# First loads of the down product moved into the last up pair, rotations moved beside the gates, six stores moved to ScalarE's queue

## The chip, the cores and the metric

The kernel runs on one core of one Trainium2 chip. The metric is the device time of one execution in microseconds (us), as the median of several runs; less is better. PE is TensorE (matmuls), PEld its weight loads, DVE is VectorE, ACT ScalarE, POOL GpSimd, and SP (SyncE) mostly issues DMAs. ACT can issue DMAs too, each in its own order of instructions. Every engine runs its instructions in order, so an instruction that waits holds up those behind it.

## The reference

One hybrid decoder block, float32, 1024 rows of width 1024 (SiLU feed-forward width 2816). Cut to what matters:

```python
h = x + 0.5 * swiglu(rms_norm(x, g1), w1a, w3a, w2a)      # (silu(x @ w1) * (x @ w3)) @ w2
u = rms_norm(h, g2)
q, k, v, p, gate_logits = split(u @ w_in)                 # one input projection, 3*768 + 512 + 2048 wide
yA = dilated_window_attention(rope(q), rope(k), v) @ w_A  # 3 groups of 4 heads, dilations 1, 4, 16
yB = pooled_minus_token(p) @ w_B                          # trailing means over 2, 4, 8, 16 rows
h = h + (sigmoid(gA) * yA + sigmoid(gB) * yB) @ w_o
h = h + 0.5 * swiglu(rms_norm(h, g3), w1b, w3b, w2b)
return rms_norm(h, g4)
```

The rotation (rope) touches the first 16 of the 64 entries of a head.

## The kernel before

**Number format and product.** Every float32 factor is split in two parts, hi and lo (ACT copies hi, DVE or POOL subtracts for lo), and a product is three matmuls: hi*hi, lo*hi, hi*lo. On top of that every large product is done in quadrants with seven products instead of eight. In the stages up and mix the seven are called m = 1, 6, 2, 7, 5, 4, 3 (`ORDER`), an item is 12 matmuls of 128x512, and products 1 and 2 share one PSUM bank, as do 5 and 3 (`Quad.run`, `Sevens.product`, L312). Sums of weights are made on DVE (`Quad.operand`, L343 to L354) and split two items ahead (`Sevens.split`, L301 on ACT, L304 on DVE or POOL).

**Weights.** `Stream` (`raws`) loads pieces of weights in one order through SP (L67, L69) into a ring of buffers `raw`; `raws.get()` takes the next and `raws.back(n)` gives n back and at once issues the loads that now have room.

**Stages.** up of the first FFN (to 457 us of the profile), down (to 680), entry and mix (684 to 1082), attention (to 1210), the product with w_o (to 1296), entry, up and down of the second FFN (1296 to 1989).

**Up and down.** `up` multiplies pairs of width blocks by w1 and w3; `Pair.a_out` and `b_out` empty the banks (b_out on DVE, L514 to L524) and `finish` spills five sums of the gated result to DRAM (`gs`, L533 on SP). `Down` multiplies these by w2 in steps of 24 matmuls: `load` fetches a spilled sum (`g`, L610, SP), `begin` takes raw weights, sums them (L646, DVE) and splits weights (`b`) and activations (`a`) (L625 on ACT; L629 on DVE, each fourth on POOL), `multiply` is L663. In `run`, step i is followed by load i+3 and begin i+2. At the end of `up`, load 0, begin 0, load 1 and begin 1 stand after the last item and before the last spills, load 2 after them.

**Mix.** 19 blocks of columns of the input projection (`MIX`), seven items each: blocks 0 to 8 are queries, keys and values, 9 and 12 pooling, 10, 11 and 13 to 18 gates. A loop over items k runs product k, then empties the bank of item k-1 in `Mix.out` (L926 to L947): of one block, DVE does m = 7 in L935 and m = 5 in L939, and product 3, two items after 5, accumulates into the bank that L939 reads. Gates end with a sigmoid on ACT (L947). What follows a block (`finish`) is a generator in the list `later`; each yield gives the number of items to wait. For queries and keys it is `rotate`: stores to DRAM on ACT's queue (`rot`, `qk`), a load of the part that is rotated (`ro`, L970), a shuffle (L974), a product with a table on POOL (L975) and one on DVE (L976), their sum (L980) and a store (L982). For gates it is `store` (L956, SP). With block 12 the tables are dropped and the attention's mask is loaded.

**Attention and w_o.** Near the end of mix the attention's inputs are fetched (`qk_in`, `pool_in`, L1547, in rings on SP). At the end of w_o, the rows h are stored to `h_dram[1]` (L1878, SP), squared on ACT (L257), and overwritten by DVE with their scaled form (L265), transposed on PE (`x_b`, L379) and split for the second FFN.

Of the kernel before, what the change touches and what calls it, by code (L numbers as in the profile page):

```python
# [27 lines left out]
GROUPS = 3  # L28
# [81 lines left out]
MIX = []  # L110
# [16 lines left out]
def tile_block(  # L127
# [31 lines left out]
    def sbuf(name, side="left", bufs=1):  # L159
        return tc.tile_pool(name=name, bufs=bufs, side=side, reuse_waits="tile")  # L160
# [156 lines left out]
    class Quad:  # L317
# [36 lines left out]
                ve.tensor_tensor(src, a12, self.s2, op=OP.subtract)  # L354
            self.w[m] = self.sv.split(src, f"{n}{m}", eng)

        def run(self, m):
            if m not in self.w:
                self.operand(m)
            w, n = self.w.pop(m), self.n  # L360
            x = {1: "b11", 2: "b21", 3: "b22", 4: "t4", 5: "t1", 6: "t2", 7: "t3"}[m]
            key = {1: "x", 2: "x", 5: "v", 3: "v"}.get(m, m)
            if m not in (2, 3):
                self.bank[key] = bank("mm" if key in ("x", "v") else "acc", f"u_{self.sv.name}{n}{m}")
            self.sv.product(self.bank[key], w, x, start=m not in (2, 3))
            if m == 3:
                raws.back(2)
            return self.bank[key]

# [15 lines left out]
    class Entry:  # L385
# [19 lines left out]
        def then(self, i):  # L405
            if i is not None:
                self.out(i)
# [139 lines left out]
            spill(6, d[:, highs])  # L547
            spill(5, d[:, lows])

    def up(sv, sums, between, at_end, begun):  # L550


        for j in range(NPAIR - 1):
            ms = [m for m in ORDER if j not in begun or m not in (1, 2)]
            q = begun.pop(j, None) or Pair(sv, j, sums)
            for m in ms:
                q.a(m)
            raws.depth = 4
            if j == NPAIR - 2:
                between()  # L560
            for m in ms[:-2]:
                q.b(m)
            if j == NPAIR - 2:
                end = Pair(sv, NPAIR - 1, sums)
                for m in ORDER[:2]:
                    end.A.operand(m)
            for m in ms[-2:]:
                q.b(m)
            q.finish()
        with tc.manual_schedule():  # L570
            items = [(w, m, out) for w, out in ((end.A, end.a_out), (end.B, end.b_out)) for m in ORDER]
            n = len(items)
            res = []
            for k, (w, m, out) in enumerate(items):
                if k + 2 < n:
                    items[k + 2][0].operand(items[k + 2][1])
                res.append(w.run(m))
                if k == n - 1:
                    then = at_end(sv.half_tile)
                if k > 0:  # L580
                    items[k - 1][2](items[k - 1][1], res[k - 1])
            then()
            end.b_out(ORDER[-1], res[-1])
            end.finish()

    def spilled(name):
        return [
# [4 lines left out]
    class Down:  # L592

        def __init__(self, name, sums, dp):
            self.name, self.sums, self.dp = name, sums, dp
            self.steps = [(m, s) for m in range(len(DOWN)) for s in range(len(PAIRS))]
            self.held, self.g, self.ops, self.banks = {}, {}, {}, {}
            self.n_lo = 0  # L600
            self.half_tile = None

        def size(self, i):
            js = PAIRS[self.steps[i][1]]
# [25 lines left out]
                at += n  # L630
            return hi, lo

        def begin(self, i):
            m, s = self.steps[i]
            pr = DOWN[m]
            size = self.size(i)
            for kn in pr.loads:
                self.held[kn, s] = raws.get()
            if len(pr.right) == 1:
                srcs = [self.held[pr.right[0], s]]  # L640
            else:
                x, y, op = pr.right
                srcs = []
                for a in range(size):
                    t = self.half_tile("s", f"w{i}_{a}").rearrange("p (a c) -> p a c", a=1)
                    ve.tensor_tensor(t, self.held[x, s][:, a:a + 1], self.held[y, s][:, a:a + 1], op=op)  # L646
                    srcs.append(t)
            w = self.split("b", srcs, i)
            for kn in pr.drops:
                del self.held[kn, s]  # L650
            raws.back(len(pr.drops))
            self.ops[i] = (self.split("a", [self.g.pop(i)], i), w)

        def multiply(self, i, t):
# [15 lines left out]
        def run(self, pool, after, tick=None):  # L670
            def half_tile(tag, n):
                return pool.tile([P, HALF], F32, tag=tag, bufs=4, name=f"{tag}_{self.name}{n}")

            self.half_tile = half_tile
            self.load(2)
            n = len(self.steps)
            done = []
            for i, (m, s) in enumerate(self.steps):
                if i < n - 2:
                    for t in range(4):  # L680
                        self.multiply(i, t)
# [159 lines left out]

    sums = spilled("f1")
    mstack, dstack = ExitStack(), ExitStack()
    down = []
    X_mix = {}

    def begin_down1(half_tile):
        scope.close()
        X_mix.update(sums_of_x(mstack.enter_context(sbuf("xa")), "mix", ("b21", "b11")))
        return begin_down("f1", half_tile)  # L850

    def begin_down(name, half_tile):
        d = Down(name, sums, dstack.enter_context(sbuf(f"down_{name}")))
        down.append(d)
        d.half_tile = half_tile
        d.load(0)
        d.begin(0)

        def then():
            d.load(1, row)  # L860
            d.begin(1)

        return then

    def load_residual():
        for t in range(NT):
# [7 lines left out]
    with sbuf("up1", "right") as fp:  # L874
        sv1 = Sevens("f1", X, fp)
        with tc.manual_schedule():
            begun = begin_up1()
        up(sv1, sums, load_residual, begin_down1, begun)
    raws.depth = RAW_BUFS


# [25 lines left out]
    class Mix:  # L907
# [44 lines left out]

        def store(self):
            yield 2
            for a in range(2):
                nc.sync.dma_start(gate_dram[self.g][:, a], self.y[a])  # L956

        def rotate(self):
            g, y = self.g, self.y
# [3 lines left out]
            for a in range(2):  # L963
                for n in range(2):
                    nc.scalar.dma_start(given[:, a, n].rearrange("t r c -> r t c"),
                                        y[a][n * HD:n * HD + 16].rearrange("r (t c) -> r t c", t=2))
                nc.scalar.dma_start(qk_dram[u][a].rearrange("h d c -> (h d) c"), y[a])
                yield 1 + a
            ro = tmp(f"ro{u}").rearrange("p (a c) -> p a c", a=2)
            nc.scalar.dma_start(ro[:, 0, :], given.rearrange("t a h r c -> (t a h r) c"))  # L970
            yield 2
# [30 lines left out]
        def window(self):  # L1002

            yield 1
            for a in range(2):
# [34 lines left out]
                for part, v in enumerate((hi, lo)):  # L1040
                    nc.sync.dma_start(pool_dram[g][:, part], v.bitcast(F32))

    pool_w_in = []

    def load_pool_w():
# [102 lines left out]
    with sbuf("steps1", "right") as pool:  # L1148
# [70 lines left out]

        raws.load()  # L1220
        with tc.manual_schedule():
            down.pop().run(pool, after1, tick)
    dstack.close()
    X_mix.update(sums_of_x(mstack.enter_context(sbuf("xb")), "mix", ("b22", "t2", "t3", "t1", "t4")))

# [13 lines left out]
    with tc.manual_schedule():  # L1239
# [4 lines left out]
        for k in range(len(items) + 4):  # L1244
# [18 lines left out]
                        later.remove(job)  # L1263
            if k == 7 * 6:
                load_pool_w()
            if k == 7 * 12:
                tables.clear()
                mask = keep.tile([P, 384], F32, tag="gain", bufs=1, name="mask")
                nc.sync.dma_start(mask, c_mask)
# [476 lines left out]

    sums = spilled("f2")

    def begin_down2(half_tile):
        x2.close()  # L1750
        return begin_down("f2", half_tile)

    pairs = [Pair(sv2, j, sums) for j in range(2)]
    entry2 = pre_run(sv2, [(q, m) for q in pairs for m in (1, 2)], pairs[0], h)
# [74 lines left out]
    with tc.manual_schedule():  # L1829
# [45 lines left out]
        hi_o(STEPS - 2)  # L1875
        for t in range(4):
            add_o(m - 2, t)
            nc.sync.dma_start(h_dram[1][t], h[t])  # L1878
            squares(t, tmp(f"square_{t}"))
        inverse(0)  # L1880
        lo_o(STEPS - 2)
# [65 lines left out]
            nc.scalar.dma_start(h[t], h_dram[1][t])  # L1947
        gains_of.append(load_gain(final_norm, "final"))

    up(sv2, sums, load_residual2, begin_down2, dict(enumerate(pairs)))  # L1950
    fs.close()
    raws.depth = RAW_BUFS
    final_gain = gains_of[1]
# [27 lines left out]
    with sbuf("steps2", "right") as pool:  # L1981
        raws.load()
        with tc.manual_schedule():
            down.pop().run(pool, after2)
    dstack.close()


# [89 lines left out]
```

## Time and profile before

| | |
|---|---|
| Runs | 1992.16, 1989.43, 1992.93 us; median 1992.16 |
| Profiled execution | 1990.87 us, of which the span is 1989.1 |
| TensorE clock granted, mean | 0.991 |
| PE busy | 1927.1 us (97%), 8966 matmuls |
| DVE, ACT, POOL busy | 1334.4 (67%), 764.0 (38%), 726.8 (37%) us |
| PE idle | some 49 us in gaps, and a slower pace after the longer ones |
| DMA | 333.57 MB, 168 GB/s in the mean |

The busy times give the engine that bounds; the waits name what ended last before an idle stretch; the timeline of one engine shows each instruction with its start, length and the idle time before it; the windows give busy times, granted clock and DMA share of a stretch.

### The profile page before, as it was taken

How to read it: one execution, taken by the hardware profiler on the slowest of the kernel's cores; microseconds unless marked ns; L12 is line 12 of the kernel's file. 1: busy time of each engine (PE TensorE's matmuls, PEld its weight loads, DVE VectorE, ACT ScalarE, POOL GpSimd, SP SyncE). 2: the span in 40 equal slices, each digit the busy share in tenths (PEclk: the TensorE clock that was granted, in tenths of full speed). 3: DMA queues.
4: the chain of work that ended last, by engine and by line, in shares of the span. 5: the costliest groups of instructions: out<-in, count | busy, mean ns of one | idle time of the engine just before them, and what ended most of it. 6: DMA issues, size and time to landing. Idle time of an engine off the chain costs nothing. (4 is left out here: it accounts for less than half of the span.)

```text
span 1989.1 us, 25124 instructions
## 1 busy us (share of the span) xinstructions
PE 1927.1 (97%) x8966; PEld 1585.2 (80%) x8966; DVE 1334.4 (67%) x2014; ACT 764.0 (38%) x1361; POOL 726.8 (37%) x555
## 2 busy tenths in 40 slices
PE   8999999998999999999998999999999999989997
PEld 7788888886888877788877888877888888868885
DVE  7766556656776775657784786768666556567776
ACT  5333333333344442334445663253323333333343
POOL 4333333331222344444544365534333333322221
PEclk9999999999999999999999999999999999999998
DMA  5323322335466527665668897653333223354664
GB/s 209 126 97 117 117 85 101 133 104 203 140 223 216 196 87 232 219 225 180 230 218 288 229 260 261 260 188 113 120 106 133 80 90 123 126 182 136 205 204 147
DMA packets 147581, 333.57 MB, mean 168 GB/s; under 512 B 20736, under 2 KB 41472, under 8 KB 145920
## 3 DMA queue, kind: packets, MB, share of 16 engines
q1 hardware_dynamic: 139104, 309.12, 46.0%
q10 hardware_dynamic: 8352, 22.85, 3.4%
q8 instruction: 71, 1.16, 0.3%
q14 instruction: 54, 0.44, 0.1%
HBM read 229.61 MB, written 102.30 MB: 167 GB/s over the span
## 5 line engine op out<-in xcount | busy, mean ns | idle before, releaser
L663 PE MATMUL d_f<-bhi_f,ahi_f 128*128 128x512 f32 x616 | 242.4, 393 | 10.4 <-ACT ahi_f L625 8.7
L663 PE MATMUL d_f<-bhi_f,alo_f 128*128 128x512 f32 x616 | 242.3, 393 | 3.0 <-POOL alo_f L629 1.9
L663 PE MATMUL d_f<-blo_f,ahi_f 128*128 128x512 f32 x616 | 241.0, 391 | 0.0
L629 POOL TENSOR_TENSOR alo_f<-g_f,ahi_f 128x512 fp32r<-128x512 f32 x70 | 97.4, 1408 | 317.1 <-ACT ahi_f L625 317.1
L312 PE MATMUL u_mixm<-xhi_t_mix,wc_mixm 128*128 128x512 f32 x608 | 195.4, 392 | 1.4 <-POOL wc_mixm L304 1.3
L312 PE MATMUL u_mixm<-xhi_b_mix,wc_mixm 128*128 128x512 f32 x456 | 150.8, 396 | 6.5 <-DVE y_m L939 5.0
L663 PEld LDWEIGHTS d_f<-bhi_f,ahi_f 128*128 128x128 f32 x616 | 116.6, 189 | 36.5 <-ACT ahi_f L625 10.4
L663 PEld LDWEIGHTS d_f<-bhi_f,alo_f 128*128 128x128 f32 x616 | 116.3, 189 | 31.4 <-POOL alo_f L629 5.4
L663 PEld LDWEIGHTS d_f<-blo_f,ahi_f 128*128 128x128 f32 x616 | 116.4, 189 | 24.0
L312 PEld LDWEIGHTS u_mixm<-xhi_t_mix,wc_mixm 128*128 128x128 f32 x608 | 113.8, 188 | 26.8 <-POOL wc_mixm L304 2.9
L312 PE MATMUL u_mixm<-xlo_t_mix,wc_mixm 128*128 128x512 f32 x304 | 118.4, 389 | 0.0
L304 POOL TENSOR_TENSOR wc_mixm<-s_mixm,wc_mixm 128x512 fp32r<-128x512 f32 x52 | 73.4, 1414 | 102.6 <-ACT wc_mixm L301 90.2
L312 PEld LDWEIGHTS u_mixm<-xhi_b_mix,wc_mixm 128*128 128x128 f32 x456 | 86.3, 189 | 26.9 <-issue 6.8
L312 PE MATMUL u_mixm<-xlo_b_mix,wc_mixm 128*128 128x512 f32 x228 | 89.4, 392 | 0.0
L625 ACT ACTIVATE ahi_f<-g_f 128x1024 fp32r<-128x1024 f32 x84 | 81.8, 974 | 4.9 <-DMA g_f<-gs_f 4.9
L301 ACT ACTIVATE wc_mixm<-s_mixm 128x512 fp32r<-128x512 f32 x76 | 47.0, 629 | 94.5 <-DVE s_mixm L345 45.9
L625 ACT ACTIVATE bhi_f<-s_f2w 128x512 fp32r<-128x512 f32 x55 | 32.9, 628 | 104.3 <-DVE s_f2w L646 96.6
L304 POOL TENSOR_TENSOR wc_mixm<-raw,wc_mixm 128x512 fp32r<-128x512 f32 x40 | 58.8, 1475 | 31.4 <-ACT wc_mixm L301 31.4
L1799 PE MATMUL wo<-w_o,o_hi 128*128 128x512 f32 x224 | 70.2, 395 | 0.0
L625 ACT ACTIVATE bhi_f<-s_f1w 128x512 fp32r<-128x512 f32 x55 | 32.9, 629 | 96.9 <-DVE s_f1w L646 92.2
L312 PEld LDWEIGHTS u_mixm<-xlo_t_mix,wc_mixm 128*128 128x128 f32 x304 | 57.1, 188 | 11.6
L1561 PE MATMUL yp<-pool_in,wab 128*128 128x512 f32 x192 | 52.9, 410 | 5.3 <-DMA pool_in<-pool 5.3
(1297 smaller groups left out, 5091.9 us busy)
## 6 DMA issues: line engine op xcount, KB each, us to landing
g_f<-gs_f SPq DMA_DIRECT2D x70, 512.0 KB, 4.7
raw<-in_w2a_dram SPq DMA_DIRECT2D x35, 512.0 KB, 4.2
raw<-in_w2b_dram SPq DMA_DIRECT2D x35, 512.0 KB, 4.1
raw<-in_w1a_dram SPq DMA_DIRECT2D x22, 512.0 KB, 4.7
raw<-in_w3a_dram SPq DMA_DIRECT2D x22, 512.0 KB, 6.1
gs_f<-y_f SPq DMA_DIRECT2D x44, 256.0 KB, 2.0
gs_f<-gb_f SPq DMA_DIRECT2D x44, 256.0 KB, 2.3
gs_f<-gd_f SPq DMA_DIRECT2D x44, 256.0 KB, 2.8
```

The source lines that it names most:

```text
L301: ac.activation(w[:, 0], src, AF.Copy)
L304: eng.tensor_tensor(w[:, 1], src, w[:, 0].bitcast(F32), op=OP.subtract)
L312: pe.matmul(p, a, b, start=(start and k == 0 and q == 0), stop=(k == 3 and q == 2), skip_group_check=not start)
L625: ac.activation(hi[:, c], src, AF.Copy)
L629: eng.tensor_tensor(lo[:, d], src[:, o], hi[:, d].bitcast(F32), op=OP.subtract)
L663: pe.matmul(self.banks[m][t], l, r, start=(first and q == 0), stop=(last and q == 2))
L1561: pe.matmul(p, a, b, start=(j == 0), stop=(j == 11))
L1799: pe.matmul(banks[m][t], l, r, start=(st == 0 and j == 0 and q == 0), stop=(st == 1 and j == 1 and q == 2))
```

## The change

1. Both FFNs: `up` makes the object `Down` before the last pair. Load 0 and load 1 are issued at its item 7; before the last-but-one item the last two buffers of weights are given back and the sums of weights of step 0 are made (new `sums_w`); after the last item come the room for `down` and begin 0; after the last `b_out` come begin 1 and load 2; the spills (`finish`) come last.
2. Mix: `rotate` ends with its stores. Load, shuffle, products, sum and store are a generator of their own, `rope`, begun at the second item (m = 6) of blocks 8, 10, 11, 13, 14 and 15. The dropping of the tables and the load of the mask move from block 12 to block 16.
3. The last gate's two stores, and four stores of h (rows 0 to 3) at the end of w_o, are issued by ACT instead of SP.

```diff
-    def up(sv, sums, between, at_end, begun):
+    def up(sv, sums, between, name, room, begun):
...
+        d = Down(name, sums, sv.half_tile)
         with tc.manual_schedule():
...
             for k, (w, m, out) in enumerate(items):
                 if k + 2 < n:
                     items[k + 2][0].operand(items[k + 2][1])
-                res.append(w.run(m))
+                if k == 7:
+                    d.load(0)
+                    d.load(1, row)
+                if k == n - 2:
+                    raws.back(2)
+                    d.sums_w(0)
+                res.append(w.run(m, k < n - 1))
                 if k == n - 1:
-                    then = at_end(sv.half_tile)
+                    d.dp = room()
+                    d.begin(0)
                 if k > 0:
                     items[k - 1][2](items[k - 1][1], res[k - 1])
-            then()
             end.b_out(ORDER[-1], res[-1])
+            d.begin(1)
+            d.load(2)
             end.finish()
+        return d
...
             self.half_tile = half_tile
-            self.load(2)
...
-    def begin_down(name, half_tile):
-        d = Down(name, sums, dstack.enter_context(sbuf(f"down_{name}")))
-        down.append(d)
-        d.half_tile = half_tile
-        d.load(0)
-        d.begin(0)
-
-        def then():
-            d.load(1, row)
-            d.begin(1)
-
-        return then
...
         def store(self):
             yield 2
+
+            queue = nc.sync if self.q < len(MIX) - 1 else nc.scalar
             for a in range(2):
-                nc.sync.dma_start(gate_dram[self.g][:, a], self.y[a])
+                queue.dma_start(gate_dram[self.g][:, a], self.y[a])
...
                 nc.scalar.dma_start(qk_dram[u][a].rearrange("h d c -> (h d) c"), y[a])
                 yield 1 + a
+
+        def rope(self):
+
+            u, g = self.hp * GROUPS + self.g, self.g
+            given, turned = rot_dram[u]
             ro = tmp(f"ro{u}").rearrange("p (a c) -> p a c", a=2)
             nc.scalar.dma_start(ro[:, 0, :], given.rearrange("t a h r c -> (t a h r) c"))
             yield 2
...
+    ROPES = dict(zip((8, 10, 11, 13, 14, 15), (q for q, (kind, _, _) in enumerate(MIX) if kind == "qk")))
...
                 load_pool_w()
-            if k == 7 * 12:
+            if k < len(items) and items[k][1] == 6 and items[k][0] in ROPES:
+                later.append([k + 1, mixes[ROPES[items[k][0]]].rope()])
+            if k == 7 * 16:
                 tables.clear()
...
             add_o(m - 2, t)
-            nc.sync.dma_start(h_dram[1][t], h[t])
+            nc.scalar.dma_start(h_dram[1][t], h[t])
             squares(t, tmp(f"square_{t}"))
```

More of the change, by code (lines that the diff above doesn't have):

```diff
@@ L355, in operand, with run @@
             self.w[m] = self.sv.split(src, f"{n}{m}", eng)
-        def run(self, m):
+        def run(self, m, back=True):
             if m not in self.w:
@@ L365, in run @@
             self.sv.product(self.bank[key], w, x, start=m not in (2, 3))
-            if m == 3:
+            if m == 3 and back:
                 raws.back(2)
@@ L592, in tile_block, with __init__ @@
     class Down:
-        def __init__(self, name, sums, dp):
-            self.name, self.sums, self.dp = name, sums, dp
+        def __init__(self, name, sums, half_tile):
+            self.name, self.sums, self.half_tile = name, sums, half_tile
             self.steps = [(m, s) for m in range(len(DOWN)) for s in range(len(PAIRS))]
@@ L600, in __init__ @@
             self.n_lo = 0
-            self.half_tile = None
+            self.right = {}
         def size(self, i):
@@ L631, in split, with sums_w @@
             return hi, lo
-        def begin(self, i):
+        def sums_w(self, i):
             m, s = self.steps[i]
             pr = DOWN[m]
-            size = self.size(i)
             for kn in pr.loads:
@@ L639, in begin @@
             if len(pr.right) == 1:
[L640 to L649, printed above, removed]
+                self.right[i] = [self.held[pr.right[0], s]]
+                return
+            x, y, op = pr.right
+            self.right[i] = []
+            for a in range(self.size(i)):
+                t = self.half_tile("s", f"w{i}_{a}").rearrange("p (a c) -> p a c", a=1)
+                ve.tensor_tensor(t, self.held[x, s][:, a:a + 1], self.held[y, s][:, a:a + 1], op=op)
+                self.right[i].append(t)
+        def begin(self, i):
+            m, s = self.steps[i]
+            if i not in self.right:
+                self.sums_w(i)
+            w = self.split("b", self.right.pop(i), i)
+            for kn in DOWN[m].drops:
                 del self.held[kn, s]
-            raws.back(len(pr.drops))
+            raws.back(len(DOWN[m].drops))
             self.ops[i] = (self.split("a", [self.g.pop(i)], i), w)
@@ L843, in tile_block, with down_room, room1 @@
     mstack, dstack = ExitStack(), ExitStack()
-    down = []
     X_mix = {}
-    def begin_down1(half_tile):
+    def down_room(name):
+        return dstack.enter_context(sbuf(f"down_{name}"))
+    def room1():
         scope.close()
         X_mix.update(sums_of_x(mstack.enter_context(sbuf("xa")), "mix", ("b21", "b11")))
-        return begin_down("f1", half_tile)
-    def begin_down(name, half_tile):
-        d = Down(name, sums, dstack.enter_context(sbuf(f"down_{name}")))
-        down.append(d)
-        d.half_tile = half_tile
-        d.load(0)
-        d.begin(0)
-        def then():
-            d.load(1, row)
-            d.begin(1)
-        return then
+        return down_room("f1")
     def load_residual():
@@ L877, in tile_block @@
             begun = begin_up1()
-        up(sv1, sums, load_residual, begin_down1, begun)
+        down = up(sv1, sums, load_residual, "f1", room1, begun)
     raws.depth = RAW_BUFS
@@ L1221, in tile_block @@
         with tc.manual_schedule():
-            down.pop().run(pool, after1, tick)
+            down.run(pool, after1, tick)
     dstack.close()
@@ L1747, in tile_block, with room2 @@
     sums = spilled("f2")
-    def begin_down2(half_tile):
+    def room2():
         x2.close()
-        return begin_down("f2", half_tile)
+        return down_room("f2")
     pairs = [Pair(sv2, j, sums) for j in range(2)]
@@ L1948, in load_residual2 @@
         gains_of.append(load_gain(final_norm, "final"))
-    up(sv2, sums, load_residual2, begin_down2, dict(enumerate(pairs)))
+    down = up(sv2, sums, load_residual2, "f2", room2, dict(enumerate(pairs)))
     fs.close()
@@ L1983, in tile_block @@
         with tc.manual_schedule():
-            down.pop().run(pool, after2)
+            down.run(pool, after2)
     dstack.close()
```

## The prediction

> **What bounds the kernel now.** I read the page first, then PE's idle times, then each place they name. The busy line:
>
> ```profile
> PE 1927.1 (97%) x8966; PEld 1585.2 (80%) x8966; DVE 1334.4 (67%) x2014; ACT 764.0 (38%) x1361; POOL 726.8 (37%) x555
> ```
>
> PE is the bound: of 1989.1 us span only some 62 are not matmul. The order of PE's instructions is the same in the changed kernel, and none is removed, so the change can only touch PE's waits and the slow pace after a wait. 0.2% of this time, 4.0 us, is about what a measurement can tell from no change. The list of waits in the four places that the change touches (microseconds in total, times, longest; windows 455 to 490, 684 to 1082, 1080 to 1105 and 1290 to 1310):
>
> ```profile
> PE d_f L663 <- ACT ahi_f L625: 5.6, 1, 5.6
> ...
> PE u_mixm L312 <- DVE y_m L939: 5.0, 4, 2.5
> ...
> PE yp L1561 <- DMA pool_in<-pool: 5.3, 2, 5.0
> ...
> PE x_b L379 <- DVE nst L261: 3.5, 1, 3.5
> ```
>
> What one such wait costs beyond itself is seen in PE's timeline at the first seam (start, length, instruction, idle before):
>
> ```profile
> 482.01 0.80 PE L663 MATMUL d_f<-bhi_f,ahi_f 128*128 128x512 f32 x1 [5.62 <-ACT ahi_f L625]
> 482.61 0.63 PE L663 MATMUL d_f<-blo_f,ahi_f 128*128 128x512 f32 x1
> ...
> 486.50 0.61 PE L663 MATMUL d_f<-bhi_f,alo_f 128*128 128x512 f32 x1
> 486.93 0.41 PE L663 MATMUL d_f<-bhi_f,ahi_f 128*128 128x512 f32 x1
> ```
>
> Until 486.9 matmuls start every 0.43 us or later, against 0.227 back to back elsewhere. The windows by stage give the clock beside it (columns: window, length, busy time of PE, PEld, DVE, ACT, POOL, then granted clock, DMA share, GB/s), here at the start of the attention:
>
> ```profile
> 1089.00:1092.00 3.00, 0.00 (x0) 0.00 (x0) 0.00 (x0) 0.89 (x4) 0.00 (x0) 0.85 0.99 344
> 1092.00:1095.00 3.00, 1.27 (x4) 0.62 (x4) 0.00 (x0) 0.00 (x0) 0.00 (x0) 0.50 1.03 313
> 1095.00:1098.00 3.00, 3.00 (x20) 2.78 (x21) 1.47 (x8) 0.39 (x1) 0.00 (x0) 0.51 0.93 192
> ```
>
> A wait of 2.46 us (757.73) is followed by matmuls at half pace worth about 1.7 us; waits of 1.41 and 1.51 us (796.57, 1006.79) by 0.1. The Trainium skill ("TensorE: Matmul & The Clock Gate", section "What's actually happening") puts the drop after an idle window of about 3.4 us. The wait of 2.46 us here already drew it, so the rows decide; by the page's figure the 0.9 us that I set below for half pace in the gate blocks would be nothing, and the sum 0.9 lower.
>
> **Seam from up to down, first FFN.** Before, step 3's raw weights (raw51) leave SP only at 474.25, behind five spill stores that wait for the last gate block; they land at 478.78, two sums and the split follow, and PE gets ahi at 482.01. After, raw51 stands ahead of the spills. Its buffers free once step 1 is split, so I issue it at about 466.5 and land it, with the 4.5 us of its before row (474.25 to 478.78), at 471; sums (1.29) end at 472.3. What is late next: the activations for step 3 (g_f, load 3) now stand on SP behind the next weight load, raw52, which waits for those sums; issued 472.7, landing 4.7 later (the page's median for g_f) at 477.4, split by ACT 1.05: PE can start at 478.5, and the low half on POOL (two tiles in 2.96) follows as before. That is 3.5 us earlier. The two small waits before it (0.36 and 1.21) go, but are given back: step 1 then waits for POOL's low half of step 1, done near 466.4 in both kernels, and ends at 470.8 against 470.65. So **−3.5**, between −6 (the wait gone) and −0.5 (load 3 a further 3 us late).
>
> **Second FFN.** Losses there are smaller: 0.57, 1.10, 0.53, 1.73, 0.62, 0.70 and a slow stretch, 8.7 us with it. Step 1 is again held by POOL's low half (to 1764.0). The weights leave 1.6 us earlier (1767.7 for 1769.35) and load 3 with them, 1769.15 for 1770.76: **−1.6**, between −4 and 0.
>
> **Rotations moved from blocks 1 to 9 to blocks 8, 10, 11, 13, 14, 15 of the mix stage.** Removed: the wait of 2.46 at 757.73 with its slow pace, about 4.3 us, and the wait of 1.41 at 796.57, about 1.7 (there the load of `ro` waits 3.8 us on ACT for the stores of `rot` and blocks the splits behind it; later, those stores have long landed). DVE's timeline shows how the first arose:
>
> ```profile
> 751.59 1.78 DVE L354 TENSOR_TENSOR s_mixm<-raw,s_mixm 128x512 f32<-128x512 f32 x1
> 753.29 0.68 DVE L935 TENSOR_TENSOR y_m<-u_mixm,y_m 128x512 f32<-128x512 f32 x1
> 753.89 0.68 DVE L980 TENSOR_TENSOR ro<-ro 128x512 f32<-128x512 f32 x1
> 754.49 1.78 DVE L343 TENSOR_TENSOR s_mixm<-raw 128x512 f32<-128x512 f32 x1
> 756.30 1.67 DVE L345 TENSOR_TENSOR s_mixm<-s_mixm,raw 128x512 f32<-128x512 f32 x1
> 758.74 0.69 DVE L304 TENSOR_TENSOR wc_mixm<-s_mixm,wc_mixm 128x512 fp32r<-128x512 f32 x1 [0.78 <-ACT wc_mixm L301]
> 759.35 0.68 DVE L939 TENSOR_TENSOR y_m<-u_mixm,y_m 128x512 f32<-128x512 f32 x1
> ```
>
> L939 reads product 5's bank, which product 3 accumulates into, and is late by the rotation's add, its shuffle and multiply just before the window, and by operations that take 1.7 us beside POOL instead of 0.68. Sum removed: −6.0.
> Added: in each new block shuffle, multiply and POOL's multiply stand between L935 and L939. The price from rows: shuffle to the next start 0.78, multiply 1.28 (818.30 to 820.36), and the next operation 1.77 instead of 0.68: 2.1 to 3.1 us. Against it stands the slack of L939's end before product 3's start, up to 1.83 us when DVE is prompt: block 8 1.83, block 10 1.83, block 11 1.16, block 13 1.55, blocks 14 and 15 0.15 each (block 14 already waits 0.57). So block 8 0, block 10 0.3, 11 1.2, 13 0.5, 14 and 15 2.0 each; DVE is 93% busy in block 13, so 0.6 is carried on; and half pace after waits of 2.0, between the rows of 1.5 and 2.46, 0.9 in all. Sum +7.5 (2 if the price falls on DVE's own idle time; 16 if each takes 3.1, blocks 14 and 15 fall to half pace, and some is carried). The later table and mask loads are SP issues of about 0.4 us without a reader near. Net **+1.5**, between −4 and +10.
>
> **The last gate's stores to ACT.** Before, SP waits for the last sigmoid until 1083.65, and behind it stand pool_in 0 and 1, issued 1084.56 and landing 1093.69 and 1098.72: the 5.04 us wait, then half pace to 1098. After, SP passes by 1078, and pool_in 0 queues straight behind its predecessor, which lands 1086.62. At 1 MB in 2.8 to 4.5 us (the spacing of such landings here) it lands at 1089.5 to 1092. On ACT two issues of about 0.4 stand ahead of the table load that the first exponentials need; PE's wait on them grows 0.8, inside the wait for pool_in. **−2.5**, between −6 (with the half pace) and +0.8 (landing unchanged, issues exposed).
>
> **Four stores of h to ACT.** Here DVE's scaling overwrites h and waits for the store to have read it:
>
> ```profile
> 1298.88 1.28 DVE L265 SCALAR_TENSOR_TENSOR h_again<-h_again,nst,gain_ffn 128x1024 f32<-128x1024 f32 x1 [4.22 <-DMA h_dram<-h_again]
> ```
>
> The first store was issued at 1289.82 behind 2 MB of weights on SP's queue and took 9.0 us. After, ACT issues it behind o_hi at 1292.1 in a queue of its own. No row shows how two full queues share; alone such a store takes 2.7 us, behind everything it would land at 1299.8. I take half the bandwidth: 1296.7. Scaling starts 2 us earlier, PE's wait falls from 3.47 to 1.4, and part of the half pace (2.9 us lost from 1300 to 1306) goes. Against it each square stands 0.4 later per store, the last by 1.6, off the path. **−2.5**, between −6 and +0.9 (1299.8 for 1298.88).
>
> **Sum.** −3.5 − 1.6 + 1.5 − 2.5 − 2.5 = −8.6 against the profiled execution, 1990.87 (its span 1989.1 and 1.77 around it): 1982.3. The median of the runs, 1992.16, lies 1.3 above that execution: 1983.6.
>
> **Rivals.** (1) *Bandwidth is the bound, the queue is not.* The DMA share is 0.80 to 1.06 around both waits, which speaks for it; the order on SP speaks against. Then both −2.5 are 0: 1988.6. The Trainium skill ("DMA: Bandwidth & Descriptors", section "Issuing engines are not separate DMA queues") says so: issuing elsewhere saves sequencer time alone. By that rule the sum would be 1988.6; its section "Queues, rings and completion order" has the queues take turns, which gives my half. (2) *The seams are given back*, by POOL's low halves or load 3 behind raw52: the two terms 0, 1988.7. For it: POOL takes 2.96 us per pair and holds step 1 in both. (3) *Slower: DVE falls behind in the gate blocks.* Its work in block 13 is 17.7 of 19.06 us, in 15 18.4 of 21.48; a rotation adds 2.7 to 3.8. If the lateness is not made up within a block, PE waits twice per block (L931 and L939) in blocks 11 to 16, 12 times about 1.5, with half pace four times, 25 us instead of 7.5: 2001.1. It turns the sum at 16.1 added, and decides for slower from 20.1. Against it: blocks 10, 14 and 17 have 24 to 36% idle DVE. (4) *The gates hide the rotations*, 2 instead of 7.5: 1978.1.
>
> **How the numbers follow.** Forecast 0.50, (4) 0.14, (1) 0.13, (2) 0.11, (3) 0.12. Faster by over 0.2% means under 1988.2: the forecast nearly whole, (4), and half of (1) and (2), which fall on the edge: 0.74. Within: the other half and some of the forecast's slow end, 0.15. Slower, over 1996.1: (3), 0.11. Range 1975 to 1994: from (4) with one set of stores at its good end (1974.6) to (1) and (2) together (1993.7); (3) is outside.
>
> **What would show it.** First seam: PE's wait before step 3 about 2 us, on ahi; if 5, rival 2. No wait at L939 in blocks 2 and 4, and new ones of about 2 us in blocks 14 and 15; L939 and L931 waits of over 16 us in all would be rival 3. yp's wait 1 to 3 us; the wait at L265 2 us; 5 and 4, as now, would be rival 1. PE busy must stay within some us of 1927; a change of PE's order would make the whole argument wrong.

## The result, and the profile after

The changed kernel takes 1999.73 us (median of 6 runs, 1996.89 to 2002.38) against 1992.55 us before (6 runs on the same chips): a ratio of 1.0039, 95% interval 1.0021 to 1.0057. It is slower by some 7 us where 8.6 us less were forecast. The profiled execution has a span of 2000.6 us (before 1989.1); it is the slowest of the six, so the two profiles lie 11.5 us apart where the medians lie 7.

PE's busy line, first on the page:

```profile
PE 1935.7 (97%) x8966; PEld 1589.0 (79%) x8966; DVE 1333.3 (67%) x2014; ACT 763.4 (38%) x1361; POOL 728.5 (36%) x555
```

PE does the same 8966 matmuls and is busy 8.6 us longer: busy time includes matmuls at half pace and those that are held up between weight load and start. The waits of PE in the same places (us in total, times, longest; the stages now lie at 455 to 495, 684 to 1092, 1089 to 1115 and 1300 to 1320):

```profile
PE d_f L678 <- POOL alo_f L640: 2.4, 3, 1.5
PE d_f L678 <- ACT ahi_f L636: 1.8, 1, 1.8
...
PE u_mixm L312 <- DVE y_m L942: 8.2, 6, 2.0
...
PE yp L1575 <- DMA pool_in<-pool: 1.5, 1, 1.5
...
PE x_b L379 <- DVE nst L261: 5.4, 2, 4.8
```

Only the third is as forecast (5.3 to 1.5). The wait before step 3 fell from 5.6 to 1.8, but a new one on POOL stands ahead of it; the evacuation's wait (L939, now L942) rose from 5.0 to 8.2; the wait for the scaled rows of h rose from 3.5 to 4.8.

Since the order of PE's instructions is the same in all kernels here, each matmul can be compared with itself: how much later it starts than in the first profile of before. The growth of that delay over a stage is what the stage costs, half pace included. In us, for the changed kernel, the four single edits, and a second profile of the kernel before, which shows what an execution alone does:

| stage (times of before) | forecast | changed | seam alone | rotations alone | gate stores alone | stores of h alone | before again |
|---|---|---|---|---|---|---|---|
| first seam, 457 to 500 | -3.5 | -0.43 | -0.84 | +0.07 | -0.37 | +0.15 | -0.61 |
| blocks 2 to 4 of mix, 757 to 798 | -6.0 | -2.11 | +0.40 | -4.16 | +0.20 | +0.13 | -1.51 |
| gate blocks, 917 to 1063 | +7.5 | +11.10 | -0.02 | +11.05 | -0.01 | -0.03 | -0.03 |
| start of attention, 1082 to 1110 | -2.5 | -2.87 | -0.65 | +0.06 | -2.49 | -1.13 | +0.36 |
| attention, 1150 to 1170 | 0 | +2.75 | +0.35 | +3.11 | +3.04 | -1.33 | +0.58 |
| end of w_o, 1290 to 1308 | -2.5 | +2.20 | +0.79 | +0.61 | +0.12 | +2.65 | -1.31 |
| second seam, 1756 to 1790 | -1.6 | +0.72 | +0.54 | -0.13 | +1.35 | -1.47 | +0.90 |

The six places that were forecast sum to +8.6 for the changed kernel, by chance the forecast with its sign turned. The remaining 2.9 of its 11.5 us are mostly the start (0.6) and the stretch from 1150 to 1170, which varies between executions; two of the experiments below bear on that.

The other stages vary too. In the profiles of this document whose kernels leave a stage alone, it differs from the first profile of before by -0.6 to +2.5 us at the first seam, -1.5 to +0.4 in blocks 2 to 4, -0.03 to +0.01 in the gate blocks, -1.3 to +0.4 at the start of the attention, -1.3 to +0.8 at the end of w_o and -1.5 to +1.4 at the second seam. So the gate blocks can be read closely, while entries under 1 us at the seams can't be told from nothing.

### The profile page after: what moved, and what is told of

The parts are those of the page before. It is cut to its first block, busy times and chain, and to the rows that moved or that the text cites. A ratio compares the mean times of both kernels' runs of the same rounds, so it can differ in the third digit from the quotient of the medians.

```text
span 2000.6 us, 25110 instructions
## 1 busy us (share of the span) xinstructions
PE 1935.7 (97%) x8966; PEld 1589.0 (79%) x8966; DVE 1333.3 (67%) x2014; ACT 763.4 (38%) x1361; POOL 728.5 (36%) x555
## 3 DMA queue, kind: packets, MB, share of 16 engines
q8 instruction: 71, 1.16, 0.2%
## 5 line engine op out<-in xcount | busy, mean ns | idle before, releaser
L304 POOL TENSOR_TENSOR wc_mixm<-s_mixm,wc_mixm 128x512 fp32r<-128x512 f32 x52 | 72.6, 1399 | 116.5 <-ACT wc_mixm L301 105.6
L301 ACT ACTIVATE wc_mixm<-s_mixm 128x512 fp32r<-128x512 f32 x76 | 46.8, 628 | 101.0 <-DVE s_mixm L345 51.2
L304 POOL TENSOR_TENSOR wc_mixm<-raw,wc_mixm 128x512 fp32r<-128x512 f32 x40 | 58.9, 1478 | 25.3 <-ACT wc_mixm L301 24.8
L656 DVE TENSOR_TENSOR s_f2w<-raw,raw 128x512 f32<-128x512 f32 x55 | 46.8, 888 | 16.8 <-DMA raw<-in_w2b_dram 16.8
```

The source lines that it names most:

```text
L301: ac.activation(w[:, 0], src, AF.Copy)
L304: eng.tensor_tensor(w[:, 1], src, w[:, 0].bitcast(F32), op=OP.subtract)
```

## The experiments

Each kernel was timed in three to five rounds beside the kernel before, except where it says otherwise.

**One part at a time.** Each of the four is before with one part of the diff shown above.

*The seam.*

> Before with the seam part alone (both FFNs). Theory A (each part costs by itself what the changed kernel's stage shows): about 0.4 us less at the first seam and 0.7 more at the second, so the same time within 1 us; PE waits for POOL's low half of step 1 (1.5 and 0.7 us) and for ahi of step 3 (about 1.8 us, about 3.9 in the second FFN). Rival B (the terms of the prediction hold and the rest is interaction of the parts): 5 us faster than before, the wait before step 3 near 2 us in both.

Ratio 0.9987 (0.9974 to 1.0000), 1988.16 against 1990.61 us. Nearer theory A: the seam wins at most a little (the interval reaches 1), not the 5.1 us of the prediction. Its waits on PE from 455 to 490:

```profile
PE d_f L678 <- POOL alo_f L640: 3.3, 4, 1.5
PE d_f L678 <- ACT ahi_f L636: 2.3, 1, 2.3
```

*The rotations.*

> Before with the rotations alone moved beside the gates. Theory A: 2 us less in blocks 2 to 4, 11 us more in blocks 11 to 16, so 8 to 10 us slower than before; new PE waits at the evacuation of product 5 in blocks 11, 13, 14, 15. Rival B: 1.5 us slower.

1.0038 (1.0021 to 1.0056), 1996.37 us. Theory A: the gate blocks alone lose 11.05 us, the same as in the changed kernel. This part by itself makes the change a loss.

*The last gate's stores.*

> Before with only the last gate's two stores on ScalarE's queue. Theory A: the wait of the pooled products falls from 5.0 to about 1.5 us, some 3 us are won by the middle of the attention, and they are lost again before its end, where the DMA queues are full and PE meets a load that has not come earlier: 0 to 1 us faster in all. Rival B: 2.5 us faster to the end of the attention and after it.

0.9989 (0.9979 to 0.9999), 1988.20 us; 2.49 us won at the start of the attention. The 3.04 us lost from 1150 to 1170 looked like theory A's price, but the same stretch loses 3.11 with the rotations alone and 2.44 in the kernel with the later loads (below), which is the kernel before unchanged up to there. So B's 2.5 us stand: in the four profiles with these stores on ScalarE the stage wins 2.5 to 3.0 us.

*The four stores of h.*

> Before with only the four stores of h on ScalarE's queue. Theory A: the first store lands about 9 us after its issue here too, since it shares the DMA engines with the weights; PE's wait grows from 3.5 to about 4.7 us and the kernel is 1.5 to 2.5 us slower. Rival B: the wait falls to 1.4 us, 2.5 us faster.

1.0012 (1.0002 to 1.0021), 1991.89 us; 2.65 us lost in the stage: theory A. The four ratios less one sum to +0.0026, within the interval of the whole change (0.0021 to 0.0057): the parts may simply add, and an interaction of a few us is neither needed nor excluded.

**Bytes or queue at the end of w_o.** The stores stay on SP, the weights wait:

```diff
-            if i == STEPS - 5:
-                raws.end = len(raws.pieces)
-                raws.depth = 4
-                raws.load()
...
             nc.sync.dma_start(h_dram[1][t], h[t])
             squares(t, tmp(f"square_{t}"))
+        raws.end = len(raws.pieces)
+        raws.depth = 4
+        raws.load()
```

> Before with the four loads of raw weights at the end of w_o issued behind the four stores of h instead of ahead of them; the stores stay on SP. Theory E (the bytes ahead of the first store in the DMA engines decide when it has read h, whichever queue issues it): the store lands within 4 us, scaling starts at 1295.5 instead of 1298.9, PE's wait falls from 3.5 to under 0.7 us, the slow pace after it goes: 4 to 6 us faster in this stage, unless the weights are late for the second FFN's entry. Rival F (the queue on SP decides and the bytes don't): the stores leave at the same time as before and land as before, no change.

0.9975 (0.9966 to 0.9985), 1984.98 us. From 1290 to 1308 it wins 5.16 us. DVE's timeline, the row that waited 4.22 us for the store before and 5.51 us in the changed kernel:

```profile
1297.19 1.29 DVE L265 SCALAR_TENSOR_TENSOR h_again<-h_again,nst,gain_ffn 128x1024 f32<-128x1024 f32 x1 [0.38 <-POOL nst L262]
```

and of the changed kernel:

```profile
1309.13 1.28 DVE L265 SCALAR_TENSOR_TENSOR h_again<-h_again,nst,gain_ffn 128x1024 f32<-128x1024 f32 x1 [5.51 <-DMA h_dram<-h_again]
```

The scaling now waits for the norm, not for a DMA: the first store lands 3.27 us after its issue, not 8.96. This run alone would also fit a delay in SP's queue; with the stores on ACT's queue and the loads ahead, in the experiment before, the first store still took 8.39 us. The two together speak for theory E: the bytes ahead of the store decide, whichever queue issues it. Stores on ACT with the loads behind them were not run.

**Where load 3 is issued.** In the seam alone, the activations of step 3 go through ScalarE, behind the splits of step 2:

```diff
-            nc.sync.dma_start(g, self.sums[DOWN[m].left][s])
+            (nc.scalar if i == 3 else nc.sync).dma_start(g, self.sums[DOWN[m].left][s])
...
-                if i + 3 < n:
+                if 0 < i < n - 3:
                     self.load(i + 3)
                 if i + 2 < n:
                     self.begin(i + 2)
+                if i == 0:
+                    self.load(3)
```

> The seam part alone, with load 3 (the activations of step 3) issued by ScalarE behind the splits of step 2 instead of by SP behind the next raw weights. Theory G (load 3 is late because it stands behind the next weights on SP): it leaves at about 469 instead of 473.8 and the waits for ahi of step 3 go: 1.9 us in the first FFN, 2.5 to 3.9 in the second; 3 to 5 us faster than the seam part alone. Rival H (GpSimd's low half and the DMA engines' load decide): step 3 waits for the weights or for the low half instead, under 1 us gained.

0.9979 (0.9967 to 0.9991), 1985.17 us. The first seam wins 5.03 us (0.84 without the edit), the second 0.29 (0.54 lost without). Load 3 leaves at 468.24, against 473.80 in the changed kernel, and PE's waits from 455 to 490 are down to

```profile
PE d_f L678 <- POOL alo_f L640: 2.1, 2, 1.5
```

Theory G holds for the first FFN. In the second PE still waits 2.96 us for ahi of step 3: there the raw weights of step 3 leave SP behind the five spills, at 1765.51, and land 6.3 us later (4.6 before), and DVE's sums wait 5.4 us for them, as in the changed kernel.

**POOL's turn.** Besides, `self.n_lo = 2` in `Down.__init__` in place of 0: POOL makes step 0's low half of the activations, not step 1's.

> The seam with load 3 from ScalarE and, besides, the count that gives each fourth split to GpSimd shifted by two, so that GpSimd makes the low half of step 0's activations and not of step 1's. Theory K (GpSimd's low half of step 1 is what gave the first gains back): the waits of 1.46 and 0.60 in the first FFN and 0.49 and 0.72 in the second go, 2 to 4 us faster than with load 3 alone. Rival L (VectorE then makes that low half late behind the spill's sums, or step 0 waits): under 1 us.

0.9977 (0.9965 to 0.9988): no better than without. The second seam wins 3.10 us (0.29 without), the first 1.08 us (5.03 without). At the first, step 1 waits 1.5 us in place of 2.1, now for ACT and DVE; but step 4, which waited for nothing, waits 0.7 us for ahi and 1.4 for POOL's low halves, and PE runs at half pace from 488 to 492 (granted clock 0.50). Rival L at the first seam: the wait moved on.

**Place within the block.** The rotations in the same gate blocks, begun one item later:

```diff
-            if k < len(items) and items[k][1] == 6 and items[k][0] in ROPES:
+            if k < len(items) and items[k][1] == 2 and items[k][0] in ROPES:
```

> Before with the rotations alone beside the same gate blocks, but begun one item later, so that shuffle and multiply stand behind product 5's evacuation on VectorE and not ahead of it. Theory C (place in VectorE's order: what costs is that the rotation stands ahead of the evacuation for which product 3 waits): the waits at that evacuation in blocks 11, 13, 14, 15 fall to those of before (1.1 us in all), some 3 to 4 us of the cost of the gate blocks go with their slow pace, and the kernel is 2 to 3 us faster than with the rotations as in the change. Rival D (VectorE's and GpSimd's work in these blocks is too much wherever it stands): the waits move to the next block's first evacuation and to GpSimd's low halves, and the stage costs the same 11 us.

1.0056 (1.0039 to 1.0073), 2000.36 us; the gate blocks lose 13.94 us. Theory C falls. PE's waits from 905 to 1092:

```profile
PE u_mixm L312 <- ACT y_m L928: 6.9, 4, 2.1
PE u_mixm L312 <- POOL wc_mixm L304: 3.9, 5, 1.0
PE u_mixm L312 <- ACT wc_mixm L301: 1.4, 1, 1.4
PE u_mixm L312 <- DVE y_m L939: 1.1, 2, 0.6
```

The waits at product 5 are those of before, as theory C said, but each came back elsewhere: at the next block's first evacuation (L928), at POOL's low halves and at the splits.

**Other blocks.** The same place, but blocks 3, 5, 6, 8, 9, 10:

```diff
-    ROPES = dict(zip((8, 10, 11, 13, 14, 15), (q for q, (kind, _, _) in enumerate(MIX) if kind == "qk")))
+    ROPES = dict(zip((3, 5, 6, 8, 9, 10), (q for q, (kind, _, _) in enumerate(MIX) if kind == "qk")))
```

> Before with the rotations alone, begun in blocks 3, 5, 6, 8, 9, 10, which VectorE leaves 24 to 61% idle, at the same place within the block as in the change. Theory D (the load of the block decides): no new wait over 0.3 us, 3 to 4 us won in blocks 2 to 4, so 3 to 4 us faster than before. Theory C (the place within the block decides): new waits at product 5's evacuation where its slack is small, block 3 (0.6), 6 (1.0) and 9 (1.0), each 1 to 2 us, so no faster than before.

1.0015 (1.0005 to 1.0024), 1991.39 us against 1989.25. 3.4 us won in blocks 2 to 4; but 2.78 lost from 798 to 917 and 1.64 to 1063, with a single new wait over 0.6 us among them (0.81 in block 12): otherwise short waits and matmuls held up by 0.1 to 0.2 us each behind late splits. Neither theory: lighter blocks bring the loss in blocks 5 and after from 11 to 4.4 us, not to nothing. The first seam, which the edit does not touch, lost 2.5 us in this profile.

**What in a rotation costs.** First, POOL's product done by DVE:

```diff
-            gp.tensor_tensor(ro[:, 1, :], ro[:, 1, :], tab[:, 1, :], op=OP.mult)
+            ve.tensor_tensor(ro[:, 1, :], ro[:, 1, :], tab[:, 1, :], op=OP.mult)
```

> The rotations alone beside the gates as in the change, but with GpSimd's multiply done by VectorE as well, so that the rotation puts no work on GpSimd. Theory I (contention: what costs is that VectorE's next operation runs 1.7 us beside GpSimd's multiply, and that GpSimd's low halves come late): each rotation costs 0.7 more on VectorE and saves about 1.1 on the next operation and 1.8 on GpSimd; the gate blocks cost 11 us less 3 to 5, the waits for GpSimd's low halves in blocks 14 to 16 go. Rival J (VectorE's time is what is short): the gate blocks cost the same 11 us or up to 2 more.

1.0016 (1.0006 to 1.0025). The gate blocks lose 8.31 us instead of 11.05, just above theory I (6 to 8) and well under rival J (11 to 13). But PE's listed waits in these blocks add up to only 0.4 us less. The other 2.3 us are pace: with the rotations alone PE fell to half pace after a wait in block 14 (granted clock 0.58 from 1002 to 1006), here nowhere. The waits for POOL's low halves in blocks 14 to 16, which theory I had go, stay (0.92, 0.39 and 1.02 us; 0.94 and 1.05 with the rotations alone). The medians, from different rounds, point the same way as the profiles (1.0016 and 1.0038), with intervals that just overlap. So that POOL's product is part of the price is likely, and how large a part stays open.

Second, the arithmetic left out: of each rotation only the load of `ro` and the store stay, so the rotation is not made.

> The rotations alone beside the gates, with their arithmetic left out: of each rotation only the load of ro and the store stay (shuffle, both products and the sum are left out, so the rotation isn't made). Theory I (the arithmetic on VectorE and GpSimd is the cost): the gate blocks cost under 1 us, the gain in blocks 2 to 4 stays, so 3 to 4 us faster than before. Rival M (the load and store on ScalarE's queue hold up the splits behind them): at least 3 of the 11 us of the gate blocks stay.

0.9978 (0.9968 to 0.9987). The gate blocks lose nothing (-0.01), and PE's waits there are those of before:

```profile
PE u_mixm L312 <- ACT y_m L928: 1.5, 1, 1.5
PE u_mixm L312 <- DVE y_m L939: 1.1, 2, 0.6
PE u_mixm L312 <- POOL wc_mixm L304: 0.7, 1, 0.7
```

So the whole price of the gate blocks is the rotation's arithmetic on DVE and POOL, and none of it ScalarE's queue. The 3.87 us won in blocks 2 to 4 stay, as with the arithmetic (4.16).

**Before, again** (profiled once more).

> The kernel before, profiled once more. If the wait of about 2 us near the end of the attention (a softmax behind the split of w_o on ScalarE, 1150 to 1170) that the changed kernel and five of the single edits show is a matter of the execution and not of the change, it may stand here too and this stretch be 2 to 3 us longer than in the first profile; if it comes from the edits, the stretch is as in the first profile within 0.5 us.

Its stretch from 1150 to 1170 is 0.58 us longer, with a new wait of 0.90 there. Kernels that are the same program up to there as before gave 0, +0.58, -1.33 and +2.44 (before, before again, the stores of h, the later loads). So a difference of up to 3.8 us comes without any edit; whether the changed kernel's 2.75 is all of that kind stays open. What PE waits for is an exponential behind ScalarE's split of w_o, which waits for POOL and that for a load.

**The parts that win, together.** The seam with load 3 from ScalarE, the gate's stores on ScalarE, the later loads; rotations as before; and the same with POOL's turn shifted.

> Before with the parts that won: the seam with load 3 from ScalarE, the last gate's stores on ScalarE, the raw weights behind the stores of h on SP; the rotations as before. If the parts add: 4.1 + 2.1 + 4.3 by the medians, so about 10 us faster than before, near 0.995. If they share a wait, less.

> The same with GpSimd's turn in the splits shifted by two. Theory K: 2 to 4 us faster than the same without the shift; rival L: no difference beyond 1 us.

1980.59 us against 1993.33, ratio 0.9930 (0.9918 to 0.9942): faster than both kernels, and a little more than the parts promised singly (0.9979, 0.9989 and 0.9975), within what their intervals allow. With POOL's turn shifted 0.9941 (0.9928 to 0.9955), no difference that these runs can tell; as above, the shift wins at the second seam (3.01 us for 0.91) and loses at the first (1.93 won for 5.23). The busy line of the first:

```profile
PE 1925.2 (97%) x8966; PEld 1584.1 (80%) x8966; DVE 1330.3 (67%) x2014; ACT 763.7 (39%) x1361; POOL 727.7 (37%) x555
```

## Why the prediction was wrong

The bound (PE's order fixed, only waits change) and the places were right. Of the six terms, one held, one had the wrong sign and was the clearest error of thought, and the others were mis-sized, all towards a gain. Of the 17 us between the forecast and the stages as measured, the rotations make 7.5 (3.6 more lost at the new place, 3.9 less won at the old one), the stores of h 4.7 and the seams 5.4.

**The stores of h: wrong sign (-2.5, measured +2.2 and +2.65).** The failed step is "I take half the bandwidth: 1296.7", with ACT's issue at 1292.1. The issue was right up to 0.9 us: the four stores begin to leave while o_hi is still running, at 1300.16, where SP would have issued the first near 1298.8. But the first store landed 8.86 us later, at 1309.03 (1300.1 in the times of before), against 8.96 us on SP before. The queues share only late. These are the packets, megabytes and share of SP's queue (q1) and of ACT's (q10) from 1302 to 1304:

```profile
q1 hardware_dynamic: 165, 0.61, 96.1%
...
q10 hardware_dynamic: 1, 0.00, 0.5%
```

The stores' data did not start for some 4 us. From 1304 to 1306 the two moved 103 and 83 packets, 0.47 and 0.34 MB: the half that the prediction took, but behind most of the bytes ahead. So the same time to land, counted from an issue 1.4 us later, puts the scaling 1.28 us later, which is the growth of the longest wait from 3.5 to 4.8. The upper bound (+0.9) foresaw nearly this, but counted the first store alone: the second landed at 1311.35, 10.8 us after its issue, and PE waited 0.6 us more. The stores had also been holding SP: w_o's next load now left at 1300.31, ahead of all but the first. That it took their part fits their longer times (10.8 to 12.1 us for 9.6 to 10.9), but no run shows it by itself. All this is rival 1 in kind, with a loss in place of its nothing. The Trainium skill ("DMA: Bandwidth & Descriptors", section "Issuing engines are not separate DMA queues") says that another issuing engine saves sequencer time alone. The trace agrees (8.86 us for 8.96), and the kernel with later loads shows the other half: where the bytes ahead of the store go, the wait goes, on the same queue.

**The gate blocks: mis-sized (+7.5, measured +11.1).** The step that failed is the term for half pace. PE's listed waits in these blocks grew by 7.1 us (3.3 to 10.4, longest first below), near the 6.6 that the prediction had for waits and carrying; the other 4 us are slower matmuls, for which it had 0.9.

```profile
PE u_mixm L312 <- DVE y_m L942: 6.3, 5, 2.0
PE u_mixm L312 <- POOL wc_mixm L304: 2.4, 3, 1.0
PE u_mixm L312 <- ACT y_m L931: 1.7, 2, 1.5
```

By block, from the first matmul of a block to that of the next, as forecast and measured: 10: 0.3 and 0; 11: 1.2 and 3.8; 12 (carried): 0 and 0.8; 13: 0.5 and 0.7; 14: 2.0 and 2.7; 15: 2.0 and 2.0; 16 (carried): 0 and 1.05. Half pace and carrying (0.9 and 0.6) stood in lump sums. Block 11 is the largest miss: its slack of 1.16 was taken whole for one rotation, but the block was late before that: its first evacuation ended 0.05 us ahead of product 2 (1.44 before), and L942 began 3.9 us after product 5's end (0.7 before); after the wait of 2.02 us there PE fell to half pace (1.46 us more). Waits at POOL's low halves in 14 and 15 (0.94, 0.41) were not priced. DVE's timeline in block 14 shows what was foreseen there:

```profile
1000.54 0.73 DVE L984 STREAM_SHUFFLE ro<-ro 128x512 f32<-128x512 f32 x1
1001.31 0.69 DVE L986 TENSOR_TENSOR ro<-ro,table_in 128x512 f32<-128x512 f32 x1
1001.91 1.76 DVE L1079 TENSOR_TENSOR raw<-raw,raw 128x512 f32<-128x512 f32 x1
1003.60 0.68 DVE L942 TENSOR_TENSOR y_m<-u_mixm,y_m 128x512 f32<-128x512 f32 x1
```

Shuffle and product stand ahead of L942. The next operation lasts 1.76 us beside POOL's product (1001.35, 1.78), but this is no new price in this block: before, it stood beside a low half of POOL's and lasted 1.73.

```profile
995.79 1.73 DVE L1067 TENSOR_TENSOR raw<-raw,raw 128x512 f32<-128x512 f32 x1
```

So here the wait grew by the shuffle and the product, 1.4 us (0.57 to 1.98). Rival 3 named the mechanism, waits twice per block and carrying, but priced it at 25 us; at 11 it would not have turned the forecast's sum alone (its point was 16.1).

**The rotations' old place: mis-sized (-6.0, measured -2.1, alone -4.2).** The failed step is that the wait of 2.46 us in block 2 goes with its cause. The cause was read rightly: before, ACT's split, for which DVE's L304 waited, had itself waited 2.63 us for DVE's sum. In the changed kernel DVE is early, and the wait is still 1.93 us (1.49 with the rotations alone):

```profile
757.75 1.35 DVE L304 TENSOR_TENSOR wc_mixm<-s_mixm,wc_mixm 128x512 fp32r<-128x512 f32 x1 [3.21 <-ACT wc_mixm L301]
759.03 0.68 DVE L942 TENSOR_TENSOR y_m<-u_mixm,y_m 128x512 f32<-128x512 f32 x1
```

DVE now sits idle for 3.21 us waiting for ACT. The row of ACT that held up this split before, and the one that does after:

```profile
758.08 0.63 ACT L301 ACTIVATE wc_mixm<-s_mixm 128x512 fp32r<-128x512 f32 x1 [2.63 <-DVE s_mixm L345]
...
756.56 0.63 ACT L1084 ACTIVATE late_hi<-raw 128x512 fp32r<-128x512 f32 x1 [4.72 <-DMA raw<-in_w_qkv_dram]
```

After, a split of late weights stands ahead of L301 in ACT's order and waits until 756.56 for its load. SP sent that group of loads from 749.16 on, before from 745.61; why later was not followed. So a second wait lay close behind the first. Besides, the slow pace of 1.7 us after the wait, which the prediction counted as won, is not certain to come (last section). Block 4's wait did go.

**The seams: mis-sized (-3.5 and -1.6, measured -0.4 and +0.7).** Two steps failed at the first. "Ends at 470.8 against 470.65": step 1 ended at 473.85, some 2.5 us late even without the 0.6 us that this execution lost at its start. It waited 1.47 and 0.73 us for POOL's low half, and PE then ran at half pace (granted clock 0.50 from 468 to 470). The low half ended at 467.86 (466.4 forecast): it now ran beside the spill's sums, and both took longer there. Before and after:

```profile
463.32 2.98 POOL L629 TENSOR_TENSOR alo_f<-g_f,ahi_f 128x512 fp32r<-128x512 f32 x2 [12.86 <-ACT ahi_f L625]
469.04 0.68 DVE L538 TENSOR_TENSOR gd_f<-y_f 128x512 f32<-128x512 f32 x1
...
464.05 3.81 POOL L640 TENSOR_TENSOR alo_f<-g_f,ahi_f 128x512 fp32r<-128x512 f32 x2 [12.98 <-ACT ahi_f L636]
464.97 1.76 DVE L538 TENSOR_TENSOR gd_f<-y_f 128x512 f32<-128x512 f32 x1
```

And load 3 left at 473.80 instead of 472.7 (0.6 of it the late start) and took 6.3 us to land instead of 4.7; issued elsewhere, it gave the first seam 4.2 us more. The prediction had named load 3 behind raw52 as next late; it priced it as one step of 3.5 us won, and nearly all of it was given back. At the second seam PE's wait before step 3 rose from 1.73 to 3.93 us. The weights left still behind the five spills, 0.4 us earlier instead of 1.6, and landed 1.3 us later than before. The whole difference there, +0.7 for the -1.6 forecast, is within what executions differ by.

**What held.** The last gate's stores: -2.5 forecast, -2.87 and -2.49 measured, with the wait at 1.5 (forecast 1 to 3) and PE's wait for the first exponentials up by 0.86 (0.8 forecast), with as much again in slower matmuls behind it, which the earlier pool_in covers.

## What to carry to other kernels

When an operation is moved to an engine that looks a third idle, price it by the slack of the queue at the place it lands in, block by block, and put a range on the slower pace after each wait; here four of six blocks paid (11, 13, 14 and 15), and lighter blocks paid less. Moving a transfer to another queue does not move the bytes ahead of it, and it lets go what the transfer had been holding back; to make one transfer early, make the others late. When the cause of a wait is removed, look for what would end last in the same place without it, and price only the difference.

## What the runs showed of the hardware

Half pace after a wait is a matter of the execution. The same wait of 2.46 us in block 2 was followed by half pace in the first profile of before (granted clock 0.59 from 761 to 764) and by none in the second (1.00), which made that stretch 1.54 us shorter; in the changed kernel a wait of 2.02 in block 11 drew it (0.72 from 937 to 941) and one of 1.98 in block 14 did not (1.00 from 1004 to 1008), while with the rotations alone the same two waits did the reverse (1.00 from 935 to 939, 0.58 from 1002 to 1006). A shorter one of 1.33 us at the start of the attention drew it as well (0.63 from 1095 to 1098). A fixed price per wait, such as the prediction's 1.7 us after 2.46, is a chance and not a cost. The Trainium skill ("TensorE: Matmul & The Clock Gate", section "What's actually happening") calls the window that the clock follows free-running; the two profiles agree with that, and its length of about 3.4 us for the drop is not what these waits show.

An operation of DVE that reads two tiles ran longer beside POOL: in block 11 the one behind the rotation took 1.76 us beside POOL's product (934.77), and 0.69 with that product made by DVE (932.86). Over the gate blocks PE's listed waits were only 0.4 us shorter that way, and DVE did six operations more.

A transfer on a second queue did not overtake what stood ahead on the first: with SP's queue full, ACT's moved 1 packet in the 2 us from 1302 to 1304 beside 165, and the first store took 8.86 and 8.39 us; with the loads behind it on the same queue it took 3.27.
